# Page attention of a hybrid decoder step: keys turned in 32x32 blocks on VectorE, logits in 32x32 tiles of TensorE, pages gathered a sequence ahead; convolution rows packed

## The chip, the cores and the metric

One core of a Trainium2 chip. The metric is the device time of one execution in microseconds (us), lower is better. A core has TensorE (PE in the rows, with its weight loads as PEld), VectorE (DVE), ScalarE (ACT), GpSimd (POOL) and SyncE (SP), each with an instruction stream of its own that it works off in order, and 16 DMA engines.

## What is computed

One decoder layer for 256 prompt tokens and 8 sample sequences of 4 tokens each, 288 token columns in all. The part that the change touches is the attention of the samples over their paged cache and the history rows of two short convolutions:

```python
z = x @ w_in                                   # branch A (B, C, h), q, k, v, indexer, two gates
# samples: scores of 1024 cached + 4 new keys, the 256 best kept, grouped-query softmax over them
logits = einsum('btkgd,btskd->btkgs', qg, k_sel) * HEAD_DIM ** -0.5      # 16 heads in 4 groups, dim 128
p = softmax(where(valid, logits, -inf)); o = einsum('btkgs,btskd->btkgd', p, v_sel)
# convolutions of width 3 over the tokens; the last two rows are outputs, the two before are inputs
y = ext[:, 0:T] * w[0] + ext[:, 1:T+1] * w[1] + ext[:, 2:T+2] * w[2];  new_state = ext[:, -2:]
```

The cache of a sequence is 8 pages of 128 keys, found by a page table; keys and values are float32, 4 heads of 128 each, so the keys of one sequence are 2 MB and the values 2 MB.

## The kernel before

The backbone is `stream`: for 512 output columns of a weight matrix it loads chunks of 256 rows (`raw`, 512 KB, issued on SP, 4 buffers), splits each half chunk into a rounded part on ACT (`wh`, L221) and the rest on DVE (`wl`, L222), both in 4 buffers, and runs three matmuls of 128x288 for each 128x128 block (L230 and L231 with `wh`, L232 with `wl`). A half chunk is 12 matmuls, a chunk 24. The streams follow each other: the columns of the indexer, K, V, Q, then the three of branch A (C, h, B, twice each), `w_a_out` and the gates, `w_attn_out`, `w_mix_out`, up and gate (11 groups of 4 column blocks), down.

Small work is written as generators in `tasks`. After each chunk `pump(rate)` runs the first generator until the yields add up to `rate`, here 2.0. `boost` gives what is issued there a higher priority. The order of instructions on each engine is then fixed by a scheduler when the kernel is built, from priorities and from its own idea of durations.

`attend_sample` is the third of these tasks, after the indexer and the prompt's attention. For each of the 8 sequences: two indirect DMAs (L289, issued on POOL) gather K pages into `kr`; 32 transposes on TensorE against the identity (L783) turn them, ACT and DVE copy them to `kts` (L752); 16 matmuls of 32 query columns (L788) on four column tiles of 32, added to a mask that a matmul with `selb` lays down (L776), give 4x256 logits at a time; DVE takes maxima (L766), ACT copies the logits to `L` (L767) and forms the exponentials (L799); nine transposes (L807, L811) turn the probabilities; 36 matmuls (L816, L825) multiply them with the gathered V pages; one more transpose (L830) puts the result into the sample columns of `Qh` and `Ql`. K and V gathers share two buffers of 1 MB.

`hist_load` brings 16 history rows of 512 columns in by DMA and turns them with four transposes of 16x128 (L865). `conv_rows` turns the 18 last rows of four column blocks with four transposes (L873) and writes them out.

## Time and profile before

| | us |
|---|---|
| median of 3 runs | 1932.89 (1932.28 to 1934.3) |
| the profiled execution | 1934.16 |
| its span, first to last instruction | 1932.4 |
| PE busy | 1890.4 (98%), 14486 matmuls |
| DVE, ACT, POOL busy | 1191.3 (62%), 873.9 (45%), 330.0 (17%) |
| sample attention on PE | from 405.7 to 727.5 |

Rows of the profile name line, engine, operation and `out<-in` by the program's tile names, then count, duration and, in brackets, how long the engine was idle before and what ended that. A float32 matmul that is not rounded to the fast format appears as two instructions. Ends of matmuls are modelled, so how far apart they start says more than how long each took.

### The profile page before, as it was taken

Reading aid. Unit: us, or ns where it says so; the run is one execution under the profiler, and the core shown is the slowest. Engines: PE = TensorE matmul, PEld = TensorE weight load, DVE = VectorE, ACT = ScalarE, POOL = GpSimd, SP = SyncE. Lnnn points to the kernel's source line nnn. Section 1 sums busy time; section 2 is a strip of 40 time slices with the busy share of each in tenths; the row PEclk is TensorE's granted clock in tenths of the full one; section 3 lists DMA queues with packets and bytes.
Section 4 is the critical chain, followed back from the end, with each engine's and each line's share of the span. In section 5 each row is a group of like instructions: output and inputs, shape, how many; then the busy total and the mean of one; then the engine's idle time right before and its main releaser. Section 6 shows DMA issues by size and latency. Waiting matters only on the chain.

```text
span 1932.4 us, 37368 instructions
## 1 busy us (share of the span) xinstructions
PE 1890.4 (98%) x14486; PEld 1816.0 (94%) x14486; DVE 1191.3 (62%) x2360; ACT 873.9 (45%) x1710; POOL 330.0 (17%) x562
## 2 busy tenths in 40 slices
PE   8999999999999999999999999999999999999997
PEld 8989999988888889999998899999999999999996
DVE  5887996745444464456578865555555556555464
ACT  4555545443443444444455544444444445333342
POOL 3331230112112111100058411110000012000000
PEclk9989999999999999999999999999999999999998
DMA  7435444466666565666554655555555555555553
GB/s 234 139 124 156 136 131 143 125 216 212 216 220 218 199 219 178 189 213 206 183 164 122 191 166 165 166 164 158 163 167 167 164 164 188 171 172 173 166 169 109
DMA packets 180802, 334.47 MB, mean 173 GB/s; under 512 B 13145, under 2 KB 44083, under 8 KB 176396
## 3 DMA queue, kind: packets, MB, share of 16 engines
q1 hardware_dynamic: 168752, 276.92, 47.3%
q0 software_dynamic: 11200, 53.99, 8.0%
q8 instruction: 114, 1.87, 0.4%
q10 hardware_dynamic: 672, 1.18, 0.2%
q14 instruction: 64, 0.52, 0.1%
HBM read 320.88 MB, written 11.17 MB: 172 GB/s over the span
## 4 chain that ended last, share of the span: by engine, by line
PE 54%; DVE 2%; issue 0%; ACT 0%; POOL 0%; DVEq 0%; ACTq 0%
PE pm L232 18%; PE pm L230 18%; PE pm L231 17%; DVE wl L222 1%; DVE big L1059 0%; PE px L1179 0%; DVE big L1235 0%; PE py L873 0%; PE py L865 0%; POOL big L1013 0%; ACT wh L221 0%; DVE u L1093 0%; DVE mv L1214 0%; DVE lnt L1055 0%; DVEq L1254 0%
## 5 line engine op out<-in xcount | busy, mean ns | idle before, releaser
L222 DVE TENSOR_TENSOR wl<-raw,wh 128x512 fp32r<-128x512 f32 (+1 forms) x1044 | 745.9, 723 | 583.8 <-ACT wh L221 577.0
L231 PE MATMUL pm<-big,wh 128*128 128x288 f32 x3728 | 1094.9, 296 | 0.0
L230 PE MATMUL pm<-big,wh 128*128 128x288 f32 x3728 | 1088.2, 297 | 1.3 <-ACT th L927 1.0
L232 PE MATMUL pm<-big,wl 128*128 128x288 f32 x3728 | 1056.3, 297 | 8.8 <-DVE wl L222 8.7
L221 ACT CAST wh<-raw 128x512 fp32r<-128x512 f32 (+1 forms) x1044 | 636.5, 619 | 788.9 <-PE pm L231 730.0
L231 PEld LDWEIGHTS pm<-big,wh 128*128 128x128 f32 x3728 | 700.8, 188 | 3.1 <-issue 2.7
L230 PEld LDWEIGHTS pm<-big,wh 128*128 128x128 f32 x3728 | 697.7, 188 | 5.9 <-issue 2.9
L232 PEld LDWEIGHTS pm<-big,wl 128*128 128x128 f32 x3728 | 683.3, 188 | 16.8 <-DVE wl L222 11.6
L232 PE MATMUL pm<-fb,wl 128*128 128x288 f32 (+1 forms) x448 | 127.6, 303 | 7.8 <-DVE wl L222 7.8
L230 PE MATMUL pm<-fb,wh 128*128 128x288 f32 (+1 forms) x448 | 134.5, 303 | 0.0
L231 PE MATMUL pm<-fb,wh 128*128 128x288 f32 (+1 forms) x448 | 133.9, 301 | 0.0
L232 PEld LDWEIGHTS pm<-fb,wl 128*128 128x128 f32 x448 | 83.5, 193 | 9.2 <-DVE wl L222 9.2
L231 PEld LDWEIGHTS pm<-fb,wh 128*128 128x128 f32 x448 | 87.1, 194 | 0.1
L230 PEld LDWEIGHTS pm<-fb,wh 128*128 128x128 f32 x448 | 86.9, 194 | 0.2
L884 POOL COPY gatf<-U 128x2 f32<-128x2 f32 x44 | 14.4, 327 | 240.5 <-ACT U L1107 236.3
L783 PEld LDWEIGHTS px<-cst,kr 128*128 128x128 f32 x256 | 29.4, 140 | 24.2 <-issue 21.5
L788 PE MATMUL px<-kts,q 128*32 128x256 f32 x256 | 46.1, 390 | 0.0
L783 PE MATMUL px<-cst,kr 128*128 128x128 f32 x256 | 44.6, 286 | 0.6 <-DMA kr<-in_cache_k_dram,pidx 0.6
L881 POOL COPY U<-hs 128x16 f32<-128x16 f32 x52 | 18.7, 377 | 138.9 <-DVE hs L867 138.4
L644 POOL TENSOR_TENSOR r<-r,rot 32x288 f32<-32x288 f32 x20 | 23.9, 1195 | 103.2 <-DVE r L643 102.7
L752 ACT COPY kts<-px 128x512 f32<-128x512 f32 x32 | 18.4, 587 | 51.2 <-PE px L783 51.2
L289 POOL DMA_INDIRECT vr<-in_cache_v_dram,pidx x16 | 15.4, 963 | 147.7 <-PE px L783 143.2
(355 smaller groups left out, 1401.8 us busy)
## 6 DMA issues: line engine op xcount, KB each, us to landing
raw<-in_w_in_dram SPq DMA_DIRECT2D x176, 512.0 KB, 3.6
raw<-in_w_up_dram SPq DMA_DIRECT2D x88, 512.0 KB, 3.7
raw<-in_w_gate_dram SPq DMA_DIRECT2D x88, 512.0 KB, 3.7
raw<-in_w_down_dram SPq DMA_DIRECT2D x86, 512.0 KB, 3.9
raw<-in_w_attn_out_dram SPq DMA_DIRECT2D x32, 512.0 KB, 3.8
raw<-in_w_mix_out_dram SPq DMA_DIRECT2D x32, 512.0 KB, 3.8
raw<-in_w_a_out_dram SPq DMA_DIRECT2D x16, 512.0 KB, 4.1
ma_d<-ya POOLq DMA_DIRECT2D x4, 576.0 KB, 3.9
```

What stands on the lines that cost most here:

```text
L221: nc.scalar.copy(wh[:, : na * ncol], part)
L222: tt(out=wl[:, : na * ncol], in0=part, in1=wh[:, : na * ncol].bitcast(F32), op=ALU.subtract)
L230: mm(o, wh[:, c : c + w], xh, start=(q == 0), stop=False)
L231: mm(o, wh[:, c : c + w], xl, start=False, stop=False)
L232: mm(o, wl[:, c : c + w], xh, start=False, stop=(q == nk - 1))
L289: nc.gpsimd.indirect_dma_start(out=dst, out_offset=None, in_=rows, in_offset=bass.IndirectOffsetOnAxis(ap=pidx[n][:, i : i + 1], axis=0))
L644: nc.gpsimd.tensor_tensor(out=t0[0:32], in0=t0[0:32], in1=C("cosq", 32), op=ALU.mult)
L752: (nc.scalar.copy if flip[0] else nc.vector.tensor_copy)(dst, src)
L783: nc.tensor.transpose(kt[:, i // 2, i % 2], raw[2 * u + i % 2][:, kv * P : (kv + 1) * P], ident)
L788: mm(lg[32 * kv : 32 * kv + 32, u * TP : (u + 1) * TP], qs[:, kv], kts[:, kv].rearrange("p a b -> p (a b)"), start=False, stop=(u == 1))
L881: nc.gpsimd.tensor_copy(sview(U, 0, 2), hs[:, i].rearrange("p (b j) -> p b j", j=2))
L884: nc.gpsimd.tensor_copy(gat[:, i, 0:2], U[:, 256:258])
```

## The change

The keys are no longer turned by TensorE. `turn` does it on DVE: a STREAM_TRANSPOSE of 128x1024 turns every 32x32 block within itself; four of them carry the keys of a sequence from the gathered pages `kg` straight to `KT`. Block (i, j) of the array, 32 keys by 32 of the 128 dimensions, is then a 32x32 tile of TensorE: 64 matmuls of 32 rows, 16 columns and 256 keys (288 for the first row group, with the new keys) on 16 tiles, each row group into a PSUM bank of its own (`lg[0..3]`, all four `px` banks). The queries have to lie in all four row groups; 16 small copies on POOL (`queries`) put them there. The mask `bms` and `selb` are laid out alike. The exponentials are taken from PSUM (L828, four of 128x256 and one of 128x32, with the sums by accumulation) and the copy of the logits goes. K and V have two gather buffers each; K of the next sequence is gathered at the head of a sequence, V after the last use of this one's. Each sequence has eight stages with a yield of 2.0 each, so one chunk of the stream lies between two stages, and the higher priority ends (`boost[0] = None`).

`hist_load` brings 16 rows of 1024 columns as a 128x128 block, for two groups at once, and turns it with one transpose (L897); `conv_rows` packs the 18 rows of four blocks to 72 and turns them with one (L905). In branch A the rows are written one chunk into the next stream.

```diff
-            for b in range(NB):
-                ...
-                        kr = sp.tile([P, GP * 512], F32, tag="pg", bufs=2, name=nm("kr"))
-                        ...
-                                nc.tensor.transpose(kt[:, i // 2, i % 2], raw[2 * u + i % 2][:, kv * P : (kv + 1) * P], ident)
-                            copy(kts[:, 2 * h : 2 * h + 2], kt)
-                        ...
-                            mm(lg[32 * kv : 32 * kv + 32, u * TP : (u + 1) * TP], qs[:, kv],
-                               kts[:, kv].rearrange("p a b -> p (a b)"), start=False, stop=(u == 1))
-                ...
-                nc.scalar.activation(L, L, AF.Exp, bias=mx[:, 3:4], scale=SCALE, accum_out=sm)
+            boost[0] = None
+            ...
+            def queries(b):
+                QB = sp.tile([P, 4, NH * TS], F32, tag="QB", bufs=1, name=nm("QB"))
+                for j in range(4):
+                    for i in range(4):
+                        nc.gpsimd.tensor_copy(QB[32 * i : 32 * i + 32, j],
+                                              qsum[32 * j : 32 * j + 32, b].rearrange("p h t -> p (h t)"))
+                return QB
+            def gather(src, b, tag):
+                ...
+                    t = sp.tile([P, GP * 512], F32, tag=tag, bufs=2, name=nm(tag))
+                    pages(t, src, GP, (b * NPG + c * 4) // GP)
+            def turn(kr, c):
+                for u in range(2):
+                    nc.vector.transpose(out=KT[:, 4 * c + 2 * u : 4 * c + 2 * u + 2].rearrange("p r k j s -> p (r k j s)"),
+                                        in_=kr[c][:, u * 1024 : (u + 1) * 1024])
+            ...
+            for b in range(NB):
+                ...
+                if not last:
+                    kr = gather(ck, b + 1, "kg")
+                lg = [psx([P, TP + NEW]) for _ in range(4)]
+                ...
+                for j in range(4):
+                    for i in range(4):
+                        o = slice(32 * i, 32 * i + 32)
+                        n = NPG + 1 if i == 0 else NPG
+                        for kv in range(NKV):
+                            mm(lg[i][32 * kv : 32 * kv + 16, : 32 * n].rearrange("p (n s) -> p n s", s=32),
+                               QB[o, j, 16 * kv : 16 * kv + 16], KT[o, :n, kv, j], start=False, stop=(j == 3))
+                yield 2.0
+                yield 2.0
+                ...
+                    nc.vector.tensor_reduce(out=mx[:, i : i + 1], in_=lg[i] if i == 0 else lg[i][:, :TP], axis=AX.X, op=ALU.max)
+                ...
+                yield 2.0
+                ...
+                    nc.scalar.activation(L[:, :NPG, 32 * i : 32 * i + 32], lg[i][:, :TP].rearrange("p (k s) -> p k s", s=32),
+                                         AF.Exp, bias=mx[:, 5:6], scale=SCALE, accum_out=sm[:, i : i + 1])
+                ...
+                yield 2.0
+                if not last:
+                    turn(kr, 0)
+                yield 2.0
+                ...
+                        nc.tensor.transpose(pp[:, j], L[:, 4 * c + j], ident)
+                    copy(L[:, 4 * c : 4 * c + n], pp)
+                if not last:
+                    turn(kr, 1)
+                    QB = queries(b + 1)
+                yield 2.0
+                ...
-    def hist_load(src, g):
-        ...
-        for i in range(4):
-            nc.tensor.transpose(ps[:, i], hr[:16, i * P : (i + 1) * P], ident[:16, :16])
+    def hist_load(src, k0):
+        ...
+        nc.tensor.transpose(ps, hr, ident)
...
-        for i in range(4):
-            nc.tensor.transpose(ps[:, i], gat[:, i], ident)
+        nc.tensor.transpose(ps, gat.rearrange("p r m -> p (r m)"), ident)
```

How the change moves instructions, at three places. On PE of the kernel before, in the logits of the first sequence, transposes of pages (L783) and logit matmuls (L788, and L795 for the new keys) alternate:

```order
L783 MATMUL px_5431<-cst,kr_5369 128x128 x2
L788 MATMUL px_5371<-kts_5373,q_896_5289 32x256
L783 MATMUL px_5431<-cst,kr_5369 128x128
L788 MATMUL px_5371<-kts_5373,q_896_5289 32x256
L783 MATMUL px_5431<-cst,kr_5369 128x128
L793 LDWEIGHTS selb
L793 MATMUL px_5477<-bms,selb 128x32
L795 MATMUL px_5477<-kn,q_896_5289 32x32 x2
L788 MATMUL px_5371<-kts_5424,q_896_5289 32x256 x2
L795 MATMUL px_5477<-kn,q_896_5289 32x32 x2
L230 MATMUL pm_5248<-big_120,wh_5404 128x288
```

On PE of the changed kernel, in the same place, the 64 logit matmuls of a sequence stand in one piece, four column tiles to a row, the four row groups in turn:

```order
L230 MATMUL pm_5255<-big_123,wh_5259 128x288
L814 MATMUL px_5501<-KT,QB_5306 16x288 x4
L814 MATMUL px_5502<-KT,QB_5306 16x256 x4
L814 MATMUL px_5503<-KT,QB_5306 16x256 x4
L814 MATMUL px_5504<-KT,QB_5306 16x256 x4
L814 MATMUL px_5501<-KT,QB_5306 16x288 x4
```

Behind them stand stream matmuls and then the nine transposes of the probabilities (L843). Between the last logit matmul and the first of these transposes stand, sequence by sequence, 53, 48, 72, 66, 48, 120, 48 and 48 stream matmuls. The 36 matmuls with V (L854) stand in 4, 5, 1, 2, 2, 1, 2 and 2 pieces, with stream matmuls between.

On DVE of the kernel before, in the first sequence, each maximum (L766) has a part of the stream's weights (`wl`) behind it:

```order
L766 TENSOR_REDUCE mx_5293<-px_5477 128x1
L222 TENSOR_TENSOR wl_5516<-raw_5497,wh_5515 128x512
L766 TENSOR_REDUCE mx_5293<-px_5371 128x1
L222 TENSOR_TENSOR wl_5566<-raw_5563,wh_5565 128x512
L797 TENSOR_REDUCE mx_5293<-mx_5293 128x1
L798 TENSOR_SCALAR mx_5293<-mx_5293 128x1
L222 TENSOR_TENSOR wl_5582<-raw_5563,wh_5581 128x512
```

On DVE of the changed kernel, in the third sequence (the first, second and fourth to seventh read alike), the four maxima and the four block transposes for the next sequence stand in one piece ahead of the maximum over the maxima (L824), and that ahead of the next `wl`:

```order
L222 TENSOR_TENSOR wl_6641<-raw_6622,wh_6640 128x512
L823 TENSOR_REDUCE mx_6657<-px_6504 128x1
L823 TENSOR_REDUCE mx_6657<-px_6505 128x1
L823 TENSOR_REDUCE mx_6657<-px_6506 128x1
L823 TENSOR_REDUCE mx_6657<-px_6507 128x1
L786 STREAM_TRANSPOSE KT<-kg_6500 128x1024 x2
L786 STREAM_TRANSPOSE KT<-kg_6502 128x1024 x2
L824 TENSOR_REDUCE mx_6657<-mx_6657 128x1
```

Behind these follow one `wl`, the scaling of the maximum (L825) that the exponentials wait for, and further `wl`. The `wl` right behind L824 is first used by PE 50 stream matmuls behind the last logit matmul (47 in the first sequence). On ACT of the changed kernel the five exponentials stand ahead of the weights of a later half chunk:

```order
L221 CAST wh_6684<-raw_6666 128x512
L828 ACTIVATE L_6656,ssm_6658<-px_6504,mx_6657 128x8x32
L828 ACTIVATE L_6656,ssm_6658<-px_6505,mx_6657 128x8x32
L828 ACTIVATE L_6656,ssm_6658<-px_6506,mx_6657 128x8x32
L828 ACTIVATE L_6656,ssm_6658<-px_6507,mx_6657 128x8x32
L830 ACTIVATE L_6656,ssm_6658<-px_6504,mx_6657 128x32
L221 CAST wh_6709<-raw_6707 128x512
```

The `wh` behind them is first used 72 stream matmuls behind the last logit matmul.

## Rows read from the trace of the kernel before

**Rows 1.** The page: PE's granted clock in 40 slices of the span.
```profile
PEclk9989999999999999999999999999999999999998
```

**Rows 2.** Busy time by stretches: engines' busy us (instructions), clock, DMA share, GB/s.
```profile
735.00:830.00 95.00, 95.00 (x719) 95.00 (x718) 45.45 (x74) 41.33 (x74) 8.44 (x16) 1.00 0.62 193
405.70:727.50 321.80, 321.17 (x2776) 268.08 (x2776) 156.94 (x310) 131.11 (x253) 48.82 (x74) 1.00 0.62 209
```

**Rows 3.** PE by lines, 405.7 to 727.5: count, busy us, mean ns, idle before.
```profile
L230 PE MATMUL pm<-big,wh 128*128 128x288 f32 x506 | 150.3, 301 | 0.0
L231 PE MATMUL pm<-big,wh 128*128 128x288 f32 x505 | 148.8, 298 | 0.0
L232 PE MATMUL pm<-big,wl 128*128 128x288 f32 x506 | 144.0, 299 | 0.0
L783 PE MATMUL px<-cst,kr 128*128 128x128 f32 x256 | 44.6, 286 | 0.6 <-DMA kr<-in_cache_k_dram,pidx 0.6
```

**Rows 4.** PE in order of time, logits of the first sequence: start us, us, instructions.
```profile
415.44 0.30 PE L231 MATMUL pm<-big,wh 128*128 128x288 f32 x1
415.89 0.62 PE L788 MATMUL px<-kts,q 128*32 128x256 f32 x2
...
419.17 0.38 PE L232 MATMUL pm<-big,wl 128*128 128x288 f32 x1
```

**Rows 5.** PE in order of time, first sequence: probabilities turned, then the V matmuls.
```profile
434.05 0.71 PE L807 MATMUL px<-cst,L 128*128 128x128 f32 x5
...
434.95 0.38 PE L230 MATMUL pm<-big,wh 128*128 128x288 f32 x1
...
438.05 0.42 PE L816 MATMUL px<-vn,ptn 32*32 32x128 f32 x8
438.40 1.95 PE L825 MATMUL px<-vr,pt 128*32 128x128 f32 x64
440.28 0.40 PE L231 MATMUL pm<-big,wh 128*128 128x288 f32 x1
```

**Rows 6.** PE in order of time, end of the first sequence's logits.
```profile
423.50 0.38 PE L788 MATMUL px<-kts,q 128*32 128x256 f32 x1
423.50 0.20 PE L795 MATMUL px<-kn,q 128*32 128x32 f32 x1
423.51 0.60 PE L788 MATMUL px<-kts,q 128*32 128x256 f32 x3
```

**Rows 7.** DVE by lines, the whole span: count, busy us, mean ns, idle before.
```profile
L222 DVE TENSOR_TENSOR wl<-raw,wh 128x512 fp32r<-128x512 f32 x1040 | 743.5, 723 | 580.7 <-ACT wh L221 574.0 <-PE pm L232 1.3 <-ACT big L241 1.1
L715 DVE TENSOR_REDUCE nmx<-px 128x1 f32<-128x256 f32 x16 | 6.6, 411 | 0.0
L766 DVE TENSOR_REDUCE mx<-px 128x1 f32<-128x512 f32 x16 | 11.1, 692 | 16.8 <-PE px L788 16.8
L377 DVE STREAM_SHUFFLE t<-t 128x288 f32<-128x288 f32 x8 | 3.7, 482 | 0.1
```

**Rows 8.** ACT by lines, 405.7 to 727.5: count, busy us, mean ns, idle before.
```profile
L799 ACT ACTIVATE L<-L,mx 128x1056 f32<-128x1056 f32 x8 | 9.4, 1179 | 0.1
L799 ACT ACTIVATION_READ_ACCUMULATOR L<-L,mx 128x1 f32 x8 | 1.5, 184 | 0.0
L767 ACT COPY L<-px 128x32 f32<-128x32 f32 x8 | 1.5, 183 | 3.1 <-DVE mx L766 3.1
```

**Rows 9.** Two waits of PE elsewhere, in order of time; idle us before, in brackets.
```profile
82.52 0.80 PE L232 MATMUL pm<-big,wl 128*128 128x288 f32 x4 [1.34 <-DVE wl L222]
1058.83 1.34 PE L232 MATMUL pm<-fb,wl 128*128 128x290 f32 x4 [3.31 <-DVE wl L222]
```

**Rows 10.** Busy time in a stretch behind the second of those waits, columns as in rows 2.
```profile
1058.80:1064.80 6.00, 5.97 (x24) 5.82 (x24) 6.00 (x6) 3.84 (x10) 5.98 (x7) 0.50 0.36 102
```

**Rows 11.** L289 from 400 to 730: time from issue to landing of a gather.
```profile
DMA to landing us min/median/max: 5.4/6.6/9.6
```

**Rows 12.** PE by lines, the whole span: the transposes of the history rows.
```profile
L865 PE MATMUL py<-cst,hr 16*128 16x16 f32 x52 | 5.6, 214 | 0.0
```

More of the change, by code (lines that the diff above doesn't have):

```diff
@@ L752, in copy @@
                 (nc.scalar.copy if flip[0] else nc.vector.tensor_copy)(dst, src)
+            boost[0] = None
+            qsum = sp.tile([P, NB, NH, TS], F32, name="qsum")
+            qh, ql = (v[:, :, TP:T].bitcast(F32).rearrange("p h (b t) -> p h b t", t=TS) for v in (Qh, Ql))
+            nc.gpsimd.tensor_tensor(out=qsum.rearrange("p b h t -> p h b t"), in0=qh, in1=ql, op=ALU.add)
+            KT = sp.tile([P, NPG + 1, NKV, 4, 32], F32, name="KT")
+            nc.gpsimd.tensor_copy(KT[:32, NPG].rearrange("p k j s -> p j k s"), kn4)
@@ new lines, in queries @@
+            def queries(b):
[6 more added lines that the diff above has]
+            def gather(src, b, tag):
+                out = []
+                for c in range(2):
+                    t = sp.tile([P, GP * 512], F32, tag=tag, bufs=2, name=nm(tag))
+                    pages(t, src, GP, (b * NPG + c * 4) // GP)
+                    out.append(t)
+                return out
@@ new lines, in turn @@
+            def turn(kr, c):
+                for u in range(2):
+                    nc.vector.transpose(out=KT[:, 4 * c + 2 * u : 4 * c + 2 * u + 2].rearrange("p r k j s -> p (r k j s)"),
+                                        in_=kr[c][:, u * 1024 : (u + 1) * 1024])
+            kr = gather(ck, 0, "kg")
+            vr = gather(cv, 0, "vg")
+            QB = queries(0)
+            yield 2.0
+            yield 2.0
+            yield 2.0
+            for c in range(2):
+                turn(kr, c)
+                yield 2.0
@@ L810, in attend_sample @@
-                pn = psx([32, P])
-                nc.tensor.transpose(pn, L[:, 1024:SL], ident)
-                copy(ptn, pn)
-                po = psx([P, P])
-                for kv in range(NKV):
-                    o = slice(32 * kv, 32 * kv + 32)
-                    mm(po[o], ptn[:, o], vn[:, kv * P : (kv + 1) * P], start=True, stop=False)
-                yield 0.5
-                for j in range(NPG):
-                    if j % GP == 0:
-                        vr = sp.tile([P, GP * 512], F32, tag="pg", bufs=2, name=nm("vr"))
-                        pages(vr, cv, GP, (b * NPG + j) // GP)
+                last = b == NB - 1
@@ new lines, in attend_sample @@
+                yield 2.0
+                yield 2.0
+                L = sp.tile([P, NPG + 1, P], F32, tag="L", bufs=1, name=nm("L"))
+                mx = sp.tile([P, 6], F32, tag="mx", bufs=1, name=nm("mx"))
+                sm = sp.tile([P, 6], F32, tag="sm", bufs=2, name=nm("ssm"))
+                nc.gpsimd.memset(L[:, NPG, NEW:], 0.0)
+                for i in range(4):
+                    nc.vector.tensor_reduce(out=mx[:, i : i + 1], in_=lg[i] if i == 0 else lg[i][:, :TP], axis=AX.X, op=ALU.max)
@@ L826, in attend_sample @@
-                    yield 0.3
-                ov = sp.tile([P, P], F32, tag="ov", bufs=1, name=nm("ov"))
-                nc.vector.tensor_scalar(out=ov, in0=po, scalar1=sm, scalar2=None, op0=ALU.mult)
+                        mm(po[o], L[:, j, o], v[:, kv * P : (kv + 1) * P], start=(j == NPG), stop=(j == NPG - 1))
+                if not last:
+                    vr = gather(cv, b + 1, "vg")
+                yield 2.0
+                ov = L[:, 0]
+                nc.vector.tensor_scalar(out=ov, in0=po, scalar1=sm[:, 5:6], scalar2=None, op0=ALU.mult)
@@ L916, with rows @@
         stream(w_in, C_H + g * 512, [128] * 4, KD, actx, evac_h, rate=R1)
[L917 to L918 removed]
+        def rows(k):
+            if k == 4:
+                conv_rows(gat, g, o_cap, o_cas)
+        stream(w_in, C_B + g * 512, [128] * 4, KD, actx, evac_b, rate=R1, pre=rows)
     ma_d = dp.tile([P, KD, T], F32, name="ma_d")
```

145 lines of the change are left out of this document (64 added, 81 removed).

## Prediction, made before the changed kernel was run

> **What bounds the kernel now.** I read the page first. PE is busy for 98% of the span (table above) and its clock is nearly always at full speed [rows 1]; DVE has 62%, ACT 45%. So time is saved by taking instructions off PE's row, and lost when PE is made to wait. Next I asked what a stream matmul costs. In a stretch with nothing else PE runs 717 of them in 95 us [rows 2] (two of the 719 counted only reach in), 0.1325 us each. The stretch of the sample attention is 321.8 us long and holds 1517 stream matmuls [rows 2, 3], 201.0 us at that price. The remaining 120.8 us are what the attention costs on PE, 15.1 us a sequence. PE waits there for almost nothing, 0.6 us ahead of L783 [rows 3]: it is price, not waiting. Where it lies is seen in order of time [rows 4]: from 415.44 to 419.17 PE does eight transposes and eight logit instructions in alternation and loses 3.6 us. Each change between a 128-wide transpose and a 32-wide tile costs a pause, and two passes of 256 keys follow each other on one tile.
>
> **The change part by part. Removed:** all 120.8 us, to be replaced by what follows.
>
> *PE work added, each sequence.* (a) Logits. A pass of 256 float32 columns takes about 0.216 us on its tile. (Three L788 span 0.60 us, one alone takes 0.38, so the last starts 0.22 behind the first [rows 6].) A tile gets 4 matmuls of two passes, the first row group 288 columns instead of 256: 8 x 0.243 = 1.94 us if the 16 tiles run side by side. No row has several row groups at work; the nearest is the four column tiles of L825, where 64 instructions of 128 columns start within 1.9 us, 0.03 us each, a quarter of what one tile would need [rows 5]. With the mask (0.2) and a pause of some 0.1 us on either side and 0.1 for the first weights, 2.5 us. The other bound is that the row groups take turns: 16 x 2 x 0.216 = 6.9 us instead of 1.94. I take the side-by-side value, since the nearest row shows it. (b) Nine transposes of probabilities as before, 434.05 to 434.95 [rows 5], 0.9 us. (c) V: 438.05 to 440.28 plus the pause ahead, 2.3 us, but cut into 19 pieces over eight sequences instead of 8, each cut some 0.35 us (two pauses and the first weights): 18.4 + 4 = 22.5 us in all. (d) The last transpose, 0.25 us. Sum over eight: 20 + 7.2 + 22.5 + 2 = 52 us, with 1 us for the stream matmuls slowed behind each piece 53 us.
>
> *The turn on DVE and the wait that it makes.* TensorE's transposes and eight copies a sequence go; four block transposes of 128x1024 come. Their cost: the shuffle of 128x288, which also moves elements between partitions, takes 0.482 us, and each further element 1.1 ns (maxima over 256 and 512 differ by 0.281 us [rows 7]), so 0.48 + 736 x 1.1 ns = 1.29 us. [...]
>
> DVE's total load hardly rises, but its order matters. After the last logit matmul DVE has four maxima (3 x 0.41 + 0.45), four transposes (5.2), the small maximum (0.15), a `wl` (0.70) and the scaling (0.15) in one row. With 0.3 us of hand-overs the `wl` is ready 7.9 us after the logits and the exponentials may start at 8.2. An exponential of 256 takes 0.4 us by the slope between 32 and 1056 elements, and 0.18 for reading its sum [rows 8]: five take 2.7 us, to 10.9. What PE has until then: the `wl` is wanted 50 stream matmuls on, at 6.6 us; the probabilities' transposes, which need all exponentials, stand 48 matmuls on (6.4 us) in the second, fifth and seventh sequence, 53 (7.0) in the first, 66 (8.7) in the fourth, later in the others. So PE, which never waited here, waits 4.5 us in three sequences. In three (third, fourth, sixth) it waits about 2.3: 1.3 for `wl` and then, since ACT's exponentials also stand ahead of the `wh` wanted at 9.5 us, about 1 more there or at the transposes. In the first it waits about 6: its second pair of K pages may be gathered only when the first turn has freed the buffers, and a gather takes 6.6 us and up to 9.6 to land [rows 11]; the last has no turn behind it and waits nothing. Sum: 3 x 4.5 + 3 x 2.3 + 6.3 = 27 us. [...]
>
> *The clock behind a wait.* Elsewhere in the trace PE waits for `wl` too. [...] For four waits of over 4 us I take 2.5 us each, for three of 2.3 us 0.8 each on average: 12 us, between 0 and 24.
>
> *Rows of the convolutions.* A set of four L865 costs some 0.44 us of PE, a single L873 0.06, by the distances of stream matmuls around them; the 52 L865 [rows 12] and as many L873, eight of them branch A's, become 7 and 13 full transposes of 0.15 and 0.1: 9 us become 3. Gain 6 us, between 3 and 8.
>
> *At nothing.* POOL's 16 copies and gathers a sequence: POOL is busy for 49 of 321.8 us [rows 2], and the queries are wanted a sequence later. DMA: the same bytes in a shorter time, 0.62 busy would be some 0.7; `raw` has four buffers. If that cover goes, weights come late, which I leave to the range. Eight stages a sequence end well ahead of the last gate stream, so no tail is left to drain.
>
> *The sum* is made against the profiled execution, 1934.2 us (span 1932.4 and 1.8 around it), 1.3 above the median of the runs: -120.8 + 53 + 27 + 12 - 6 = -35, so 1899.4, and 1898 beside the median; I say 1899.
>
> **The rivals.** *(R1) The waits come, the clock stays up*, since they are shorter than worked out or PE's matmuls around them suffice: 1887. For it: only one of the two waits [rows 9] dropped it. *(R2) Hardly any waits*, because DVE turns a block in half the time or so: 1860 to 1872. Against it: the shuffle's rate. [...] *(R4, the other side) The row groups take turns*, one at a time through the array: 5.0 us more a sequence, 40 in all: 1939, slower than before. It decides from 4.4 us more a sequence on, since 35 us are to be eaten. For it: no row shows two row groups at once; against it: column tiles do run at once. *(R5) The block transposes run at half the rate*: waits of 60 instead of 27 us, 1932, no change.
>
> **How the numbers follow.** Forecast (1890 to 1911) 0.47; R1 (1878 to 1890) 0.18; R2 0.07; R3 (1911 to 1922) 0.10; R4 (1932 to 1945) 0.09; R5 (1922 to 1940) 0.09. The range 1872 to 1936 holds the forecast, R1, R3, a part of R2 and R5 and little of R4, some 0.85. Faster by over 0.2% (below 1929), about what a measurement of this kernel can tell from no change: forecast, R1, R2, R3 and a part of R5, 0.82 by the cases; as several of the prices have no row, I put 0.80. Within 0.2%: half of R5, a part of R4, 0.08. Slower: 0.12.
>
> **What would show it.** Right: the L814 of a sequence start within some 2 us; PE's waits name ACT's L828 before L843 and DVE's `wl` before L232, some 27 us in all; STREAM_TRANSPOSE near 1.3 us; half-clock stretches between 405 and 700 us; the attention's excess over 0.1325 us a stream matmul falls from 121 to about 92 us. Wrong: an L814 block of 3.7 or 7 us (R3, R4), no waits at L843 (R2), a clock of 1.00 throughout (R1), waits for `raw` or `kg` (the DMA cover is gone).

## The result and the profile after

The changed kernel takes 1889.34 us in the median (1888.61 to 1890.62), beside 1933.12 us for the kernel before: 43.8 us less, a ratio of 0.9774 with a 95% interval of 0.9757 to 0.9791. The forecast was 1899, from 1890 to 1911. The profiled execution took 1888.61 us, with a span of 1886.8 us.

The page of the changed kernel, busy time and granted clock, to be read beside [rows 1]:

```profile
PE 1826.9 (97%) x14954; PEld 1787.0 (95%) x14954; DVE 1209.6 (64%) x2377; ACT 851.0 (45%) x1718; POOL 373.0 (20%) x691
PEclk9989999999999999999998999999999999999998
```

PE has 468 instructions more than before (14954 for 14486) and 63.5 us less of busy time: many small tiles that run beside each other (the 128 logit instructions of the third sequence start within 2.5 us) took the place of fewer that ran one behind the other.

Where the time went is seen by cutting the span where the sample attention begins and ends. Busy time by stretches, with the clock in the third number from the end; the first two lines are the changed kernel, the last two the kernel before:

```profile
405.70:711.10 305.40, 290.36 (x3491) 269.16 (x3490) 179.60 (x343) 119.25 (x281) 84.15 (x196) 0.97 0.67 235
711.10:1886.80 1175.70, 1151.42 (x8608) 1143.54 (x8607) 705.92 (x1243) 528.60 (x996) 176.46 (x338) 0.99 0.54 171
...
405.70:730.80 325.10, 324.46 (x2801) 271.38 (x2801) 158.53 (x314) 133.19 (x258) 49.24 (x75) 1.00 0.62 208
730.80:1932.40 1201.60, 1178.38 (x8799) 1167.63 (x8798) 712.85 (x1260) 536.80 (x1007) 179.95 (x348) 0.99 0.56 170
```

The stretches do not hold the same amount of streaming, so their lengths can't be subtracted. What can be is the loss of PE: the length of a stretch less 0.1325 us, the price of a stream matmul from [rows 2], for each one started in it (both kernels have 12528). Ahead of the attention the loss goes from 94.1 to 96.7 us, in the attention from 121.1 to 82.9, behind it from 57.2 to 47.3. The attention gave 38.2 us, the part behind it 9.9, the part ahead took 2.6 (some 2 of them are more waiting of PE there). All experiments below are read by this loss too, since it comes from one trace and not from a comparison of chips.

PE by lines in the attention of the changed kernel (count, busy us, mean ns, idle before it), to be read beside [rows 3], and all that PE waited for there:

```profile
L230 PE MATMUL pm<-big,wh 128*128 128x288 f32 x561 | 169.1, 306 | 0.0
L814 PE MATMUL px<-KT,QB 32*16 32x256 f32 (+1 forms) x1024 | 25.5, 407 | 4.1 <-POOL QB L772 2.6 <-issue 1.5
L854 PE MATMUL px<-vg,L 128*32 128x128 f32 x512 | 19.1, 274 | 0.0
L843 PE MATMUL px<-cst,L 128*128 128x128 f32 x72 | 10.6, 294 | 5.1 <-ACT L L828 5.1
```

```profile
PE px L843 <- ACT L L828: 5.1, 3, 2.1
PE pm L232 <- DVE wl L222: 3.9, 1, 3.9
PE px L814 <- POOL QB L772: 2.6, 1, 2.6
PE pm L231 <- issue: 1.8, 1, 1.8
PE px L814 <- issue: 1.5, 1, 1.5
```

Five sources, 14.9 us in all, where the kernel before had 0.6. "Issue" means that the trace names nothing that PE waited for. The 256 page transposes of [rows 3] are gone. A typical sequence, the third, shows the new chain. PE in order of time (start, us, instructions):

```profile
509.50 0.29 PE L232 MATMUL pm<-big,wl 128*128 128x288 f32 x1
509.73 0.33 PE L808 MATMUL px<-bms,selb 32*32 32x288 bf16 x16
509.86 2.85 PE L814 MATMUL px<-KT,QB 32*16 32x256 f32 x128
512.64 0.40 PE L230 MATMUL pm<-big,wh 128*128 128x288 f32 x1
```

All logits of a sequence take 3.0 us out of the stream (from 509.50 to 512.64, less one stream matmul of 0.13); the 128 instructions start within 2.5 us, the 2.85 less the last one's 0.37. In the kernel before a quarter of them took 3.6 us with their page transposes [rows 4]. DVE and ACT behind that:

```profile
512.60 1.45 DVE L823 TENSOR_REDUCE mx<-px 128x1 f32<-128x288 f32 x4 [1.56 <-PE px L814]
513.97 4.61 DVE L786 STREAM_TRANSPOSE KT<-kg 128x1024 f32<-128x1024 f32 x4
518.51 0.12 DVE L824 TENSOR_REDUCE mx<-mx 128x1 f32<-128x4 f32 x1
518.54 0.68 DVE L222 TENSOR_TENSOR wl<-raw,wh 128x512 fp32r<-128x512 f32 x1
519.14 0.15 DVE L825 TENSOR_SCALAR mx<-mx 128x1 f32<-128x1 f32 x1
```

```profile
519.38 0.48 ACT L828 ACTIVATE L<-px,mx 128x256 f32<-128x256 f32 x1 [2.76 <-DVE mx L825]
...
521.19 0.30 ACT L830 ACTIVATE L<-px,mx 128x32 f32<-128x32 f32 x1
```

The row that the prediction described is there: four maxima, four block transposes, one `wl`, the scaling. The exponentials start 6.7 us behind the logits, not 8.2, and end at 8.9, not 10.9 (6.6 and 8.8 in the second, sixth and seventh sequence). A block transpose takes 1.15 us here (4.61 for four), 1.21 by itself.

The granted clock falls four times in the attention. Busy time by stretches, the clock again third from the end:

```profile
413.40:420.20 6.80, 6.80 (x107) 4.43 (x108) 1.64 (x4) 0.62 (x1) 4.93 (x16) 0.50 0.48 167
430.50:433.90 3.40, 2.76 (x13) 2.76 (x14) 2.33 (x6) 3.40 (x12) 1.70 (x2) 0.51 0.57 178
546.50:549.90 3.40, 3.40 (x16) 3.20 (x14) 3.08 (x4) 0.15 (x1) 2.46 (x11) 0.50 0.85 331
590.90:594.30 3.40, 3.40 (x16) 3.40 (x15) 3.23 (x6) 1.59 (x5) 2.92 (x4) 0.50 0.90 338
```

17.0 us at a granted clock of 0.50 or 0.51, half clock below. Most stream matmuls start 0.24 us behind one another there, instead of 0.1325, so at most 8.5 us are lost (in the second stretch PE also waits for 0.6 us). Each stretch begins behind a wait of PE: between two starts of matmuls 3.0 us pass from 410.3 on, 4.2 from 424.9, 1.9 from 544.2, 2.4 from 587.0. Two gaps of the same size, 2.3 us at 483.2 and 2.1 at 651.2, were followed by no drop.

### The profile page after: what moved, and what is told of

Read it like the earlier page. It is cut to its first block, busy times and chain, and to the rows that moved or that the text cites. A ratio compares the mean times of both kernels' runs of the same rounds, so it can differ in the third digit from the quotient of the medians.

```text
span 1886.8 us, 38417 instructions
## 1 busy us (share of the span) xinstructions
PE 1826.9 (97%) x14954; PEld 1787.0 (95%) x14954; DVE 1209.6 (64%) x2377; ACT 851.0 (45%) x1718; POOL 373.0 (20%) x691
## 3 DMA queue, kind: packets, MB, share of 16 engines
q8 instruction: 117, 1.92, 0.4%
## 4 chain that ended last, share of the span: by engine, by line
PE 85%; DVE 7%; issue 3%; DMA 2%; POOL 1%; ACT 1%; SPq 0%; DVEq 0%; ACTq 0%; POOLq 0%
PE pm L232 27%; PE pm L230 27%; PE pm L231 26%; DVE wl L222 3%; PE px L854 1%; PE px L814 1%; DMA vg<-in_cache_v_dram,pidx 1%; DMA raw<-in_w_in_dram 1%; PE px L843 1%; DVE big L1097 0%; DMA kg<-in_cache_k_dram,pidx 0%; DVE r L650 0%; PE px L534 0%; DVE big L242 0%; ACT wh L221 0%
## 5 line engine op out<-in xcount | busy, mean ns | idle before, releaser
L232 PE MATMUL pm<-big,wl 128*128 128x288 f32 x3728 | 1054.1, 297 | 13.2 <-DVE wl L222 13.0
L232 PEld LDWEIGHTS pm<-big,wl 128*128 128x128 f32 x3728 | 684.6, 188 | 19.1 <-DVE wl L222 17.3
L232 PE MATMUL pm<-fb,wl 128*128 128x288 f32 (+1 forms) x448 | 127.0, 301 | 9.5 <-DVE wl L222 9.5
L232 PEld LDWEIGHTS pm<-fb,wl 128*128 128x128 f32 x448 | 82.6, 191 | 11.2 <-DVE wl L222 11.0
L1207 POOL DMA_DIRECT2D hq<-h_d x8 | 4.4, 552 | 197.8 <-DVE r L1212 197.8
L772 POOL COPY QB<-qsum 32x64 f32<-32x64 f32 x128 | 30.5, 238 | 60.0 <-PE px L814 35.7
L786 DVE STREAM_TRANSPOSE KT<-kg 128x1024 f32<-128x1024 f32 x32 | 37.2, 1213 | 3.7 <-DMA kg<-in_cache_k_dram,pidx 3.7
L289 POOL DMA_INDIRECT vg<-in_cache_v_dram,pidx x16 | 20.5, 1280 | 61.2 <-PE px L854 45.6
L814 PE MATMUL px<-KT,QB 32*16 32x256 f32 (+1 forms) x1024 | 25.5, 407 | 4.1 <-POOL QB L772 2.6
```

The costliest lines, as they stand in the source:

```text
L232: mm(o, wl[:, c : c + w], xh, start=False, stop=(q == nk - 1))
L289: nc.gpsimd.indirect_dma_start(out=dst, out_offset=None, in_=rows, in_offset=bass.IndirectOffsetOnAxis(ap=pidx[n][:, i : i + 1], axis=0))
L772: nc.gpsimd.tensor_copy(QB[32 * i : 32 * i + 32, j], qsum[32 * j : 32 * j + 32, b].rearrange("p h t -> p (h t)"))
L786: nc.vector.transpose(out=KT[:, 4 * c + 2 * u : 4 * c + 2 * u + 2].rearrange("p r k j s -> p (r k j s)"), in_=kr[c][:, u * 1024 : (u + 1) ...
L814: mm(lg[i][32 * kv : 32 * kv + 16, : 32 * n].rearrange("p (n s) -> p n s", s=32), QB[o, j, 16 * kv : 16 * kv + 16], KT[o, :n, kv, j], star ...
```

## Experiments

In the experiments the kernel before took between 1934.8 and 1936.0 us in the median, so they are compared by their ratio to it; the changed kernel's is 0.9774.

**The rows of the convolutions alone** (the kernel before with the new `hist_load`, `conv_rows` and their callers, the attention untouched):

```diff
-        for i in range(4):
-            nc.tensor.transpose(ps[:, i], gat[:, i], ident)
+        nc.tensor.transpose(ps, gat.rearrange("p r m -> p (r m)"), ident)
```

> The kernel before with the packed convolution rows alone: history and output rows turned with one 128x128 or 72x128 transpose, the attention as it was. Behind the attention the stream of the changed kernel loses 10.2 us less than that of the kernel before to other things than its matmuls (47.3 against 57.5 us over 0.1325 us a matmul). Theory A (the rows are worth what their excursions cost, 7.6 us behind the attention becoming 0.5, and some 1.5 us more in front): 1924 to 1926 us. Theory B (part of the 10.2 us is the different fall of waits and clock, and the rows are worth the 3 to 6 us of the prediction): 1927 to 1930 us. Theory C (nothing, PE hides it): 1933 us.

1925.9 us, ratio 0.9947 (0.9930 to 0.9963), 10 us less. The stretch behind the attention:

```profile
731.40:1923.90 1192.50, 1166.94 (x8729) 1159.17 (x8727) 714.06 (x1255) 535.03 (x1007) 180.03 (x343) 0.99 0.56 171
```

It lost 48.0 us against 57.2 before and 47.3 in the changed kernel, the attention 121.8 against 121.1. So the rows are worth all that the stretch behind the attention gained: theory A. By the distances of the stream matmuls around them the excursions to L865 and L873 there cost 7.6 us and their successors 0.5, so 7.1 us of the 9.2 are theirs. Half-clock time near 1060 us fell from 13.6 to 6.8 us, 3.4 us of loss, but PE's waits behind the attention grew by 2.5 us (those for `wl` from 11.6 to 14.9). Why both moved, whether by the transposes that are gone or by another spacing of the waits, no run tells.

**The row groups one behind the other** (the two loops of the logits exchanged):

```diff
-                for j in range(4):
-                    for i in range(4):
+                for i in range(4):
+                    for j in range(4):
```

> The changed kernel with the two loops of the logits exchanged, so that the 16 matmuls of one row group stand together and the row groups follow each other; same instructions, same data. Theory A (the 16 tiles run side by side only because matmuls of all four row groups stand next to each other): a row group alone needs 16 matmuls on four tiles, 8 passes a tile of some 0.22 to 0.24 us, 1.9 us, four of them 7.5 us instead of the 2.5 us measured: 5 us a sequence, 40 us in all, 1925 to 1932 us, with an L814 block of 7 to 8 us. Theory B (the order does not matter, the time is that of issuing 128 instructions): 1889 us, block 2.5 us.

1898.58 us, ratio 0.9804 (0.9787 to 0.9820). PE in order of time, third sequence:

```profile
512.02 5.05 PE L814 MATMUL px<-KT,QB 32*16 32x288 f32 x128
```

Neither theory had it. The block does grow, so the row groups do run beside each other in the changed kernel and the order of the instructions decides how far. But it grows by 2.2 us, not by 5: the 128 instructions start within 4.7 us. The starts one by one show why. The eight passes of the first row group (288 columns) start 0.243 us apart, those of the second (256 columns) 0.216 us apart, the price of a pass that was read from [rows 6]. But the second group starts 1.00 us into the block, when 12 of the first group's 32 instructions have not started yet, and the third and fourth at 2.2 and 3.1 us: even in this order a row group does not wait until the one ahead of it is through. The loss in the attention rises by 11.3 us and not by 8 x 2.2 = 17.6, since waits went: the first maxima now run while PE is still at the logits, the exponentials come 0.85 us sooner behind them, the 3.9 us for `wl` in the first sequence and the 3.3 us put down to issue are gone, and against that stand 3.4 us more at half clock, 1.7 us of loss.

**Half the keys** (as many matmuls with 128 instead of 256 or 288 columns; the kernel leaves out the scores of the other keys and of the new ones):

```diff
                         for kv in range(NKV):
+                            n = 4
                             mm(lg[i][32 * kv : 32 * kv + 16, : 32 * n].rearrange("p (n s) -> p n s", s=32),
```

> The changed kernel with the logit matmuls over the first 128 keys of a row group alone instead of 256 or 288: the scores of the other cached keys and of the new keys are left out, the number of instructions is the same (128 on PE and as many weight loads a sequence). In the changed kernel the block takes 2.5 us from its first to its last start. Theory A (the block is bound by the columns that each of the 16 tiles has to pass): about half, 1.2 to 1.4 us. Theory B (it is bound by bringing in 128 weight loads and matmuls, 19.5 ns each; the columns of the 16 tiles run beside each other): 2.1 to 2.5 us. The waits of PE put down to issue stay by B and may go by A.

The third sequence's logits:

```profile
513.18 1.90 PE L815 MATMUL px<-KT,QB 32*16 32x128 f32 x128
```

First to last start is 1.6 us, between the two theories: halving the columns takes a third off, so neither the columns nor the count of instructions is the bound by itself; 12.7 ns an instruction, on the mean of a block, is the least that was seen. With 256 columns 78 of the 127 starts follow the one before by 15 to 18 ns, and five gaps of 0.10 to 0.18 us stand between them, where 128 columns leave one of 0.10; what sets the 15 to 18 ns stays open. The waits put down to issue did not go, they grew to 4.1 us at L815 and 2.6 at L232. The time, 1886.35 us, tells little: it comes from two executions, and the planner (the scheduler that fixes the order of instructions when the kernel is built) also laid the first sequences differently, so that one `wl` wait of 6.5 us came in.

**Block transposes held back.** A small copy into `KT` that each pair of transposes has to follow, behind the sums of the exponentials and behind the turned probabilities:

```diff
                 if not last:
+                    nc.vector.tensor_copy(KT[:, 0:4:2, 0, 0, 0], sm[:, 5:6].to_broadcast([P, 2]))
                     turn(kr, 0)
...
                 if not last:
+                    nc.vector.tensor_copy(KT[:, 4:8:2, 0, 0, 0], L[:, NPG, 0:1].to_broadcast([P, 2]))
                     turn(kr, 1)
```

> The changed kernel with the block transposes held back on VectorE by a small copy that they have to follow: the first pair behind the sums of the exponentials, the second pair behind the turned probabilities; in the second to seventh sequence the scaling of the maximum then follows the maxima at once. Theory A (the waits of PE ahead of the probabilities' transposes, 5.1 us, and what half clock follows them come from this order): both go in the second to seventh sequence, 4.2 us of waits and 1.7 us of clock less, 1882 to 1885 us; PE's waits that are put down to issue (1.5 and 1.8 us) and the first sequence's 2.6 us for the queries stay. Theory B (the waits only move to the next wl or to the logits that need the turned keys): 1888 to 1891 us.

1882.75 us, ratio 0.9724 (0.9708 to 0.9740), which does not touch the changed kernel's interval. DVE in the third sequence, then PE's three largest waits in the attention:

```profile
508.87 1.45 DVE L823 TENSOR_REDUCE mx<-px 128x1 f32<-128x288 f32 x4 [1.56 <-PE px L814]
510.35 0.16 DVE L824 TENSOR_REDUCE mx<-mx 128x1 f32<-128x4 f32 x1
510.55 0.15 DVE L825 TENSOR_SCALAR mx<-mx 128x1 f32<-128x1 f32 x1
513.05 0.16 DVE L832 TENSOR_REDUCE ssm<-ssm 128x1 f32<-128x5 f32 x1 [2.35 <-ACT L L830]
```

```profile
PE px L814 <- POOL QB L772: 2.8, 1, 2.8
PE px L814 <- issue: 1.9, 1, 1.9
PE pm L232 <- issue: 1.4, 1, 1.4
```

No wait at the transposes of probabilities is left, and the wait of 3.9 us for `wl` in the first sequence went too. The loss in the attention falls by 6.4 us, from 82.9 to 76.5. In the second and fifth sequence 48 stream matmuls stand between logits and transposes as in the changed kernel, the exponentials end at 3.8 and 4.0 us behind the logits instead of 8.8 and 8.9, and the waits of 2.0 and 2.1 us are gone. That these waits came from the block transposes ahead of the scaling is shown: theory A. (The planner also moved other things, among them the logits of the second sequence, which now stand in three pieces.)

**Every block transpose twice:**

```diff
                 for u in range(2):
-                    nc.vector.transpose(...)
+                    for _ in range(2):
+                        nc.vector.transpose(...)
```

> The changed kernel with every block transpose on VectorE done twice, 4.6 us of VectorE more in seven sequences, nothing else. This prices a wait made by VectorE. Theory A (what VectorE does between the maxima and their scaling delays the exponentials and the next wl, and PE waits for what lies beyond its cover of 48 to 72 stream matmuls): sequences 2, 5 and 7 wait 4.6 us more, the first 4.6, the third and fourth about 3.5, the sixth about 3, together 28 us, and with some 5 to 12 us of half clock behind them 1922 to 1930 us. Theory B (PE's buffers absorb it, VectorE is only 60 per cent busy there): within 5 us of the changed kernel, 1889 to 1894 us.

1896.92 us, ratio 0.9800 (0.9784 to 0.9817); the loss in the attention is 89.4 us, 6.5 more than in the changed kernel, where A had 28 and B at most 5. The eight transposes of DVE in the third sequence, and PE's three largest waits:

```profile
514.07 4.61 DVE L787 STREAM_TRANSPOSE KT<-kg 128x1024 f32<-128x1024 f32 x4
...
518.64 2.35 DVE L787 STREAM_TRANSPOSE KT<-kg 128x1024 f32<-128x1024 f32 x2
...
521.50 2.35 DVE L787 STREAM_TRANSPOSE KT<-kg 128x1024 f32<-128x1024 f32 x2
```

```profile
PE pm L232 <- DVE wl L222: 8.7, 9, 1.5
PE py L906 <- DVE yb L947: 5.7, 1, 5.7
PE pm L230 <- DVE U L935: 5.4, 1, 5.4
```

The exponentials do come later, 11.1 us behind the logits instead of 6.6. But the planner knew of the longer transposes when it laid out PE, and set 84 to 120 stream matmuls ahead of the probabilities' transposes in the third to seventh sequence, where 48 to 72 stood in four of these. So this run prices a slower turn that is planned for, at 6.5 us, and not the one of the prediction's rival, slower than planned. That was not tried.

**Higher priority kept** (`boost[0] = None` taken out):

```diff
-            boost[0] = None
```

> The changed kernel with the higher priority kept (boost stays at 1500), one line undone. The matmuls with V then stand in 8 pieces instead of 19, a sequence follows the next every 111 to 118 stream matmuls instead of 168 to 329, and between logits and the transposes of probabilities stand 53, 75, 72, 48, 64, 68, 75 and 30 stream matmuls. Theory A (each cut of the V matmuls costs 0.33 us, waits ahead of the transposes go where 64 or more matmuls cover them): 3.6 us for the cuts and some 3 us of waits less, ratio 0.974. Theory B (the DMA engines cannot bring 4 MB of pages beside the stream in some 21 us, PE waits for kg, vg or raw): ratio 0.979 to 0.99, with such waits in the trace.

1895.62 us, ratio 0.9796 (0.9780 to 0.9813). PE's two largest waits between 405.7 and 707 us (its attention ends at 607):

```profile
PE pm L232 <- DVE wl L222: 10.4, 4, 3.4
PE px L813 <- POOL QB L771: 2.7, 1, 2.7
```

Theory B's ratio, but hardly its reason: PE names neither pages nor `raw`. With all of an attention issued first, the three `wl` that PE waits for in the attention stand behind block transposes on DVE, and only the first of those was itself late, by 3.1 us in which DVE waited for `kg`. Over as many stream matmuls as the changed kernel has in its attention, 1678, this one loses 88.1 us, 5.2 more, and 5.1 of loss come from the clock, 27.3 instead of 17.1 us at half. Theory A's part can be read off all the same: the V matmuls in 8 pieces instead of 19 cost 17.5 us of PE instead of 21.4, 0.35 us a cut, and 0.2 us is left of the waits ahead of the transposes.

**Priority for logits and V alone**, through a `with tc.high_priority(1500):` around each of the two:

> The changed kernel with a higher priority for the logits and the matmuls with V alone: V in 8 pieces instead of 19, all logits still in one piece each, sequences at irregular distances (up to 192 stream matmuls between logits and transposes in one, 48 in three). Theory A (a cut costs 0.33 us): 3.6 us less, ratio 0.9755. Theory B (a cut costs nothing, since the pauses at either side are paid by the logits and transposes anyway): 0.9774.

1885.11 us, ratio 0.9743 (0.9727 to 0.9759); loss in the attention 79.6 us, 3.3 less. The pieces of V cost 17.5 us here too, so the cuts are worth what theory A said.

**Three attempts on the waits of the first and the fourth sequence.** The query copies ahead of the gathers in the source:

```diff
+            QB = queries(0)
             kr = gather(ck, 0, "kg")
             vr = gather(cv, 0, "vg")
-            QB = queries(0)
```

> The changed kernel with the 16 query copies of the first sequence issued on GpSimd ahead of the first gathers instead of behind them; nothing else. In the changed kernel PE waits 2.6 us for them in the middle of the first logits, and a stretch of 6.8 us at half clock follows. Theory A (that wait is only an order on GpSimd): the 2.6 us and up to 3.4 us of clock go, 0.14 to 0.32 per cent less time than the changed kernel, a ratio to the kernel before of 0.9743 to 0.9760. Theory B (the first gathers start 4 us later for it, their keys are turned later, and the first logits wait for these instead): ratio 0.9772 to 0.9785.

1888.85 us, ratio 0.9762 (0.9746 to 0.9778). The planner put the copies behind the gathers again, the fifth copy waits for all four of them to land, and PE still waits 2.7 us: not a test of either theory, as the order did not change.

V gathered in its own sequence, four stages ahead of its use:

```diff
-            vr = gather(cv, 0, "vg")
...
                 nc.vector.reciprocal(sm[:, 5:6], sm[:, 5:6])
+                vr = gather(cv, b, "vg")
...
-                if not last:
-                    vr = gather(cv, b + 1, "vg")
```

> The changed kernel with V of a sequence gathered in its own fourth stage, behind the exponentials, instead of at the end of the sequence before, so that the 2 MB of K and the 2 MB of V are asked for half a sequence apart and not right behind each other. The two waits of PE that are put down to issue (1.5 us within the logits of the fourth sequence, 1.8 us behind those of the seventh) end when a 16 KB block of instructions has landed that was fetched at 543.7 and 650.9 us, while the DMA share was 0.9 to 1.0. Theory A (PE waits for its instructions because the gathers fill the DMA engines): both go, with the half clock behind the first (1.7 us), 4 to 5 us, ratio 0.9748 to 0.9756. Theory B (the block comes late for another reason, such as 288 instructions in 3 us): no change, 0.977 to 0.978. Theory C (V now comes late): PE waits for vg at L854, ratio above 0.979.

1889.89 us, ratio 0.9762 (0.9745 to 0.9778); the waits put down to issue are still there, 2.1 and 0.9 us, as theory B said. Theory A is not refuted by that: from 2 us ahead of each wait to its end the DMA share was still 0.93 and 1.00, so V gathered later did not relieve the DMA engines at these places.

The queries of the first sequence on DVE, with the block transposes held back:

```diff
-                        nc.gpsimd.tensor_copy(QB[32 * i : 32 * i + 32, j],
+                        (nc.gpsimd if b else nc.vector).tensor_copy(QB[32 * i : 32 * i + 32, j],
```

> The kernel with the block transposes held back behind the exponentials, and with the queries of the first sequence copied on VectorE instead of GpSimd, where the fifth copy had to wait for the first four gathers. Theory A: beside the 6.4 us of the held-back transposes the wait of 2.7 us in the first logits goes, and the half clock of 6.8 us behind it: 6.1 us, ratio to the kernel before of 0.9690 to 0.9705. Theory B (the first logits come earlier, are cut into four pieces, and the second sequence's keys, whose gather lands when it did, are waited for instead): ratio 0.9715 to 0.973.

1882.98 us, ratio 0.9732 (0.9715 to 0.9748), no better than 0.9724 without it. The wait for the queries is gone, and another stands in its place:

```profile
PE px L808 <- ACT cb L930: 5.6, 1, 5.6
```

Theory B in its sign, though what is waited for is ACT's `cb`, not the second sequence's keys. Both with a higher priority for logits and V:

> The same with a higher priority for the logits and the matmuls with V, which brings V from 19 pieces to 9 and leaves 48 stream matmuls or more between logits and transposes of probabilities in all sequences but the first (38). Theory A (gains add up): another 3.5 us, ratio 0.967 to 0.969. Theory B (the irregular distances make gathers late, PE waits for kg, vg or wl): 0.9705 or above.

1883.4 us, ratio 0.9731 (0.9714 to 0.9747): the gains do not add up. The same 5.6 us stand in the first sequence, and 4.8 us of waits for a DVE result of L242 came in ahead of L809.

**Logits in two halves**, 24 stream matmuls apart, with the block transposes held back:

```diff
                 for j in range(4):
+                    if j == 2:
+                        yield 2.0
                     for i in range(4):
```

> The kernel with the held-back block transposes, and with the 64 logit matmuls of a sequence in two halves, 24 stream matmuls apart, so that PE has to take in its instructions less fast. In the kernel with the held-back transposes PE waits 1.9 us (fourth sequence) and 1.4 us (behind the seventh) for no semaphore, each time ending some 1.3 us after a 16 KB block of instructions has landed. Theory A (the burst of logits uses up the instructions that PE has at hand): no wait put down to issue in the second to eighth sequence, 3.3 us less, up to 1.7 us of half clock less, against seven more cuts of 0.35 us, 2.5 us more: 1879 to 1883 us, ratio 0.971 to 0.9725. Theory B (the blocks come late for another reason): the waits stay and the cuts are added, ratio 0.9735 or above.

1879.77 us, ratio 0.9715 (0.9699 to 0.9731), the lowest of all runs, though its interval overlaps those of the other three with the transposes held back. All of PE's waits in its attention:

```profile
PE px L816 <- POOL QB L772: 2.9, 1, 2.9
PE pm L232 <- DVE wl L222: 2.0, 2, 1.0
PE pm L230 <- ACT wh L221: 1.1, 1, 1.1
PE px L846 <- ACT L L830: 0.4, 1, 0.4
```

None is put down to issue, as theory A said, and the loss in the attention is 73.7 us, 2.8 less than with the held-back transposes alone.

## Why the prediction held, and which of its terms did not

The direction, the place and the mechanism were right, and the range held the time; the forecast's own band, from 1890, missed it by 0.7 us. The sum came out 10 us too high, with errors of both signs. Measured numbers are those of the two profiled executions, 1934.2 and 1888.6 us:

| term of the sum, us | forecast | measured |
|---|---|---|
| attention of the kernel before, given up | -120.8 | -121.1 |
| PE work put in its place | 53 | 59.5 |
| waits of PE | 27 | 14.9 |
| half clock | 12 | 8.5 |
| rows of the convolutions, behind the attention | -6 | -9.9 |
| ahead of the attention | 0 | 2.6 |
| sum | -35 | -45.5 |

The work is what is left of the loss of 82.9 us without waits and clock.

*Waits, the term that was most wrong.* The chain on DVE and ACT was right link by link and each link a little too long: maxima 1.34 us behind the logits where 1.7 and the hand-overs were taken, since the first runs before the last logit has ended; a block transpose 1.15 us where the shuffle's rate gave 1.29; an exponential with its sum 0.45 where 0.58 was taken. Together the exponentials were done at 8.8 us, 2.1 sooner. Against a cover of 6.4 us, the 48 stream matmuls that PE has until then, that halves a wait of 4.5 us (measured 2.0 and 2.1 in the second and fifth sequence; in the seventh the 1.8 us put down to issue stand in its place, since the transposes of probabilities start there 8.6 us behind the logits as in the other two), and it wipes out the waits of 2.3 us in the third, fourth and sixth: `wl` was ready in time in six of seven sequences. Half of the 14.9 us stand in the first sequence: 3.9 for `wl` and 1.0 at L843, where 6.3 were forecast, and 2.6 for the queries, which the forecast put at nothing. It did not have the waits put down to issue either, of which the 1.5 us in the fourth sequence came on top.

*Clock.* Four stretches, 8.5 us instead of 12; two of them, 10.2 of the 17.0 us, stand in the first sequence. The 2.5 and 0.8 us that the forecast puts behind a wait are the author's estimate, which no run shows. In the kernel before, the wait of 3.31 us [rows 9] was followed by at least 6.0 us at 0.50 [rows 10], 3.0 us of loss, and that of 1.34 us by none (the clock is 1.00 from 82.5 to 90.0 us); in the changed kernel four waits were followed by 6.8, 3.4, 3.4 and 3.4 us at half clock, at most 3.4 and three times 1.7 us of loss. Rival R1, the clock stays up, fell, though the time lies in its band: it is there because the waits were shorter, which is the other half of R1's condition.

*PE work.* The V matmuls cost 21.4 us against 22.5, and 0.35 us for a cut was right. The logits cost 3.0 us and not 2.5, 4 to 5 us over eight sequences: the block starts within 2.5 us where 1.94 were taken. The price of a pass was right: the first five passes of the first row group start 0.243 us apart in the changed kernel too. What is not reached is the full overlap of 16 tiles, as the experiment with half the columns shows, where the block shrinks by a third only (from 2.5 to 1.6 us). Stream matmuls slowed behind the cuts were put at 1 us; by the distances of stream matmuls with nothing between them they lose 4.6.

*Side by side or in turn.* In the changed kernel the row groups run beside each other, so R4 fell as the course of events: within the first 10 ns of the third sequence's block four instructions of the first row group (288 columns) and four of another (256 columns) start. The experiment shows that its price of 40 us was too high as well. In turn gave a ratio of 0.9804, about 1895 beside 1933.1, and not 1939, so even this order would not have made the kernel slower. The 0.216 us for a pass held there; the error was that row groups in turn would exclude each other. R3, a second pass that holds up the next row group, was put at a block of 3.7 us, 17 passes of 0.216 us by the author's estimate. The measured 2.5 us speak against it, and so do the starts: the first row group's second passes start 0.24 us after the other group's first ones. In the run with the row groups in turn the second row group starts when 12 of the 32 instructions of the first, all ahead of it in the loops, have not.

*R2 and R5.* Waits at L843 are there, so R2 fell. Transposes at half the rate, R5, put at some 60 us of waits (28 of them, 1.2 to 1.3 us longer each, on top of the 27), are excluded by the 1.15 us.

*Rows.* 9.9 us behind the attention against 3 to 8. The excursions, 7.1 us, lie within the bounds. What moved besides was not in the sum: the clock near 1060 us gave 1.7 us (10.2 us at half instead of 13.6), PE's waits took 1.3, and some 2.4 us stay without a cause.

*Cover.* The changed kernel's DMA share in the attention is 0.67, up from 0.62, and PE's waits name neither `raw` nor pages. In the first sequence the cover was gone all the same, one engine further back. On POOL the query copies waited for the first V pages to land, and the gathers of the second sequence's keys went out behind these copies; on DVE the block transposes then waited for those keys, with the next `wl` behind them:

```profile
413.06 3.40 POOL L772 COPY QB<-qsum 32x64 f32<-32x64 f32 x12 [10.27 <-DMA vg<-in_cache_v_dram,pidx]
416.74 0.97 POOL L289 DMA_INDIRECT kg<-in_cache_k_dram,pidx  x1 [0.28 <-POOL QB L772]
422.37 2.37 DVE L786 STREAM_TRANSPOSE KT<-kg 128x1024 f32<-128x1024 f32 x2 [2.43 <-DMA kg<-in_cache_k_dram,pidx]
426.04 2.37 DVE L786 STREAM_TRANSPOSE KT<-kg 128x1024 f32<-128x1024 f32 x2 [1.31 <-DMA kg<-in_cache_k_dram,pidx]
```

So PE's 2.6 us for `QB`, and 3.7 us of DVE's time ahead of the `wl` that PE waited 3.9 us for, are waits for gathered pages. The prediction had the gather as the reason of the first sequence's wait, and was right there.

## What to carry to other kernels

When work leaves a full engine, ask what the receiving engine has queued around it: the block transposes were cheap and DVE had room, but where they stood, ahead of a small scaling that everything else hung on, cost 6.4 us that a small dependency gave back. Follow a wait back past the engine that it names: PE named POOL and DVE in the first sequence, and behind both stood gathers. Price a chain by what its last link is wanted for and add up its links from the closest rows, because with 6.4 us of cover an error of 2 us in a chain of 10 halves the wait. Here a cut of the V matmuls cost 0.35 us (17.5 us in 8 pieces, 21.4 in 19), so count the pieces in the order of instructions, not the matmuls.

## What the runs showed of the hardware

PE stops at times without a wait that the trace names. In the changed kernel it does so between 544.6 and 546.1 us, amid the logits of the fourth sequence, and waits for no semaphore:

```profile
543.19 1.40 PE L814 MATMUL px<-KT,QB 32*16 32x288 f32 x52
546.09 0.69 PE L814 MATMUL px<-KT,QB 32*16 32x256 f32 x7 [1.49 <-issue]
```

Instructions come in by DMA, as the page's queues show (packets, MB, share of the 16 engines):

```profile
q8 instruction: 117, 1.92, 0.4%
```

Each packet is 16 KB (1.92 MB in 117). One of them started at 543.7 and took 1.05 us, another at 650.9 and 0.93; PE went on 1.3 and 1.5 us behind their landing. In all runs with the new attention, every stop of over 0.6 us in it without a semaphore stood amid logits or began at most 3.0 us behind their last start, and ended 1.2 to 1.5 us behind such a landing. There are none where the logits are slower (row groups in turn) or in two halves, and they are longest where the logits are faster (half the columns: 6.7 us in all). From 2 us ahead of each such stop to its end the DMA share was 0.87 to 1.02. With the row groups in turn and with two halves it reached 0.94 to 1.02 around the end of the logits of two sequences each, without a stop, so a full DMA alone does not make one; whether it takes part is open: in the changed kernel the six sequences without a stop have 0.41 to 0.83 there. That PE lacked instructions in these stops was the author's reading; no run shows what ends them.

A wait of about 2 us can be followed by a lower clock: of the gaps of 1.9, 2.1, 2.3 and 2.4 us, those of 1.9 and 2.4 were followed by 3.4 us at 0.50, at most 1.7 us of loss, and the two others were not. What tells them apart was not settled.
